# Filling TensorE's waits with unread products, and three changes of order, in a two-layer MoE network on one core

## The chip, the cores and the metric

The kernel runs on one core of a Trainium2 chip. The metric is device time of one execution in microseconds (us), lower is better. PE is TensorE (matrix products and transposes), DVE is VectorE, ACT is ScalarE, POOL is GpSimd, and SP is SyncE, which here only issues DMA transfers.

## The reference

Five hundred and twelve tokens of width 1024 pass through two layers and then two further blocks:

```python
for layer in range(DEPTH):                       # DEPTH = 2
    mix = gdn_mixer(h, ...) if layer == 0 else nsa_mixer(h, shared, ...)
    h = layer_norm(DEEPNORM_ALPHA * h + mix, ...)
    ffn = hier_moe(h, ...)                       # 16 experts, hidden 256, top 2
    h = layer_norm(DEEPNORM_ALPHA * h + ffn, ...)
x = second_block(h, ...)                         # twice: SGU, MLA, band attention, gated sum

def hier_moe(x, w_grp, b_grp, w_rt, b_rt, w_gate, w_up, w_down):
    grp_p = softmax(xt @ w_grp + b_grp)          # 4 groups: take the best
    e_logits = (xt @ w_rt + b_rt)[best group]    # 4 experts in it: take two
    gate = ...                                   # weights of the two, zeros elsewhere
    for wg, wu, wd, ge in experts:
        acc += ge[:, None] * ((silu(xt @ wg) * (xt @ wu)) @ wd)
```

## The kernel before

All weights are read from HBM in pieces of 512 KB (`chunk`, line 98), issued by SP into a ring of raw tiles; where a stage has spare tiles they are lent to the ring. Each piece is split into two reduced-precision parts: `hi` by an ACT cast (line 109) and `lo` by a DVE subtraction (line 110; in the experts POOL does it for the last of the four pieces of the first product, `c == 3`). Three matmuls (lines 114 to 116, or line 973 in the experts) then give the product of full precision. PE's stages follow one another without a choice: a tile scheduler keeps the written order of each engine except where priorities or `issue_after` move a row, and semaphores tie the engines together.

The start: SP loads the transposed input (`xT`, eight pieces, line 1761), a few constants, and the first mixer weights `g_w`. POOL builds a table of attention biases in `XT` with 32 small copies (line 1124), and SP writes it back to HBM as `n_fwd` (line 1126). PE first multiplies by the small weights `g_ab` (result in `br`), then by `g_w` (`mm<-xh,hi`).

Each layer's MoE: the logits of four token tiles (line 753, 128 x 20, eight of them a tile, each two PE instructions in the trace) go to DVE, where `dispatch` finds two experts per token (mask `M`, line 791), ranks, and the table `itok` of token numbers per expert. POOL gathers the rows of an expert by indirect DMA (`xr<-hd`, line 927), PE transposes them (line 189), and the branch of line 863 skips an overflow path. Every expert has a first product (`up`, four pieces), silu and product (lines 977 and 978, tile `sg`), a transpose of `sg`, and a second product (`down`, two pieces, results `yo`), which POOL adds to `acc` in HBM by an indirect DMA (`scatter`, line 932). PE runs `up(e)` before `down(e-1)`. Every scatter waits for the one before to land. The last two experts' results do not go by HBM: `combine` multiplies them by one-hot matrices (line 1054), adds `acc` (line 1057), and normalizes.

PSUM banks are shared by tag: four for `mm`, two each for `tp` and `br`.

Of the kernel before, what the change touches and what calls it, by code (L numbers as in the profile page):

```python
# [10 lines left out]
F32 = mybir.dt.float32  # L11
F32R = mybir.dt.float32r
BF = mybir.dt.bfloat16
I32 = mybir.dt.int32
U32 = mybir.dt.uint32
AF = mybir.ActivationFunctionType
OP = mybir.AluOpType
# [48 lines left out]
class Net:  # L66
    def __init__(self, ctx, tc, I, out, dbg):
# [12 lines left out]
        self.pows = self.cst.tile([128, 32], F32, name="pows")  # L80
        nc.vector.memset(self.pows, -0.5)
        self.flip = self.turn = self.turn2 = 0
        self.more, self.pairs = [], []
# [42 lines left out]
    def psum(self, tag="mm", shape=(128, 512), dtype=F32):  # L126
        return self.ps.tile(list(shape), dtype, name=tag, tag=tag, bufs=self.banks[tag])

    def copy(self, dst, src):
# [574 lines left out]
class Moe:  # L704


    def __init__(self, net, cx, l):
        self.net, self.l = net, l
        nc, tc = net.nc, net.tc
        self.mp = mp = cx.enter_context(tc.tile_pool(name="moe", bufs=1))  # L710
        self.wr = mp.tile([128, 160], F32, name="wr")
        nc.gpsimd.dma_start(self.wr, net.I[f"m_r{l}"])
        self.br = mp.tile([128, 20], F32, name="br")
# [8 lines left out]
        self.ws = mp.tile([128, 16], F32, name="ws")  # L722
        self.slots = net.psum("br")
        self.hT = []
# [25 lines left out]
    def logits(self, t):  # L750
        net = self.net
        for k in range(8):
            net.nc.tensor.matmul(self.slots[:, 64 + t * 20:84 + t * 20], lhsT=self.hT[t][:, k], rhs=self.wr[:, k * 20:k * 20 + 20],
                                 start=k == 0, stop=k == 7)

    def dispatch(self):
# [10 lines left out]
        def first_max(src, oh):  # L767
# [13 lines left out]
        x, e2, o1, o2 = (s(NT, 5, 4) for _ in range(4))  # L781
        V.tensor_tensor(x.rearrange("p t g e -> p t (g e)"), self.slots[:, 64:144].rearrange("p (t c) -> p t c", c=20),
                        self.br.unsqueeze(1).to_broadcast([128, NT, 20]), op=OP.add)
# [4 lines left out]
        for k, o in enumerate((o1, o2)):  # L788
            V.tensor_tensor(self.E2[:, k].rearrange("p t (g e) -> p t g e", e=4), o[:, :, 1:5],
                            og.unsqueeze(3).to_broadcast([128, NT, 4, 4]), op=OP.mult)  # L790
        V.tensor_tensor(self.M, self.E2[:, 0], self.E2[:, 1], op=OP.add)
        rk = net.psum("br", (128, NT, 128))
        for t in range(NT):
            for u in range(t + 1):
                PE.matmul(rk[:, t, :16], lhsT=net.ones_bf if u < t else net.tri_bf, rhs=self.M[:, u],
                          start=u == 0, stop=u == t)

        cv = self.cv
# [48 lines left out]
    def overflow(self):  # L847
# [5 lines left out]
        for u in range(NT):  # L853
            PE.matmul(cp[:, :16], lhsT=net.ones_bf, rhs=self.M[:, u], start=u == 0, stop=u == NT - 1)
        cm = mp.tile([128, 1], F32, name="cmx")
        V.tensor_reduce(cm, cp[:, :16], axis=AX.X, op=OP.max)
# [95 lines left out]
    def experts(self, aside=lambda: None):  # L952
        net, mp = self.net, self.mp
        nc = net.nc
        V, S, G, PE = nc.vector, nc.scalar, nc.gpsimd, nc.tensor
# [3 lines left out]
        def operand(k, tag, src, ps="tp"):  # L959
# [5 lines left out]
            return h, l, [lambda b=b: step(b) for b in range(0, k, 4)]  # L965

        def up(e, xh, xl, steps):

            pg = net.psum()
            for c in range(4):  # L970
                hi, lo = net.chunk(w[e, c], eng=G if c == 3 else None)
                for j, (a, b, k) in enumerate([(xh, hi, 0), (xl, hi, 0), (xh, hi, 1), (xl, hi, 1), (xh, lo, 0), (xh, lo, 1)]):
                    PE.matmul(pg, lhsT=a[:, c * 2 + k], rhs=b[:, k * 512:k * 512 + 512], start=c + j == 0, stop=c == 3 and j == 5)  # L973
                if steps:
                    steps.pop(0)()
            sg = mp.tile([128, 256], F32, name="sg", tag="sg", bufs=2)
            S.activation(sg, pg[:, :256], AF.Silu)
            V.tensor_tensor(sg, sg, pg[:, 256:512], op=OP.mult)
            return operand(2, "h", sg, "br")

        def down(e, hh, hl):
# [7 lines left out]
            for c in range(2):  # L989
                cs = slice(c * 512, c * 512 + 512)  # L990
                hi, lo = net.chunk(w[e, 4 + c])
                py = net.psum()
# [20 lines left out]

        self.ys, self.ots = [], []
        with net.longer(*self.places()):
            self.rows(XR - 1)
            x = [operand(8, "xe", self.xr[0])]
            for s in x[0][2]:
# [19 lines left out]
    def combine(self, done):  # L1038
# [9 lines left out]
        for t, r in enumerate(rt):  # L1048
            sm2, sm, ss, rs = small("sm2", 2), small("sm"), small("ss"), small("rs")
            ps = [net.psum() for _ in range(2)]  # L1050
            for j, (ot, y) in enumerate(zip(self.ots, self.ys)):
                for c in range(2):
                    for i in range(2):
                        PE.matmul(ps[c], lhsT=ot[:, t], rhs=y[i][:, c * 512:c * 512 + 512], start=j + i == 0, stop=j == DIRECT - 1 and i == 1)
            for c in range(2):
                cs = slice(c * 512, c * 512 + 512)
                V.scalar_tensor_tensor(r[:, cs], ps[c], 1.0, r[:, cs], op0=OP.mult, op1=OP.add, accum_out=sm2[:, c:c + 1])
# [681 lines left out]
def tile_network(ctx: ExitStack, tc: tile.TileContext, I, out, dbg=()):  # L1739
# [15 lines left out]
    xt = net.xt_pair()  # L1755
    net.phase(mm=4, tp=2, br=2)
    g_small = gdn_small(net)
    for j in range(4):
        xx = net.ring.tile([128, RING], F32, name="raw", tag="raw", bufs=RAW)
        for u in range(2):  # L1760
            nc.sync.dma_start(xx[:, u * T:u * T + T], I["xT"][2 * j + u])
        v = xx.rearrange("p (k t) -> p k t", k=2)
# [52 lines left out]
```

## Time and profile before

| | before |
|---|---|
| median of 3 runs | 2187.76 us (2184.25 to 2189.46) |
| profiled execution, time | 2186.32 us |
| profiled execution, span | 2184.6 us |
| mean granted TensorE clock | 0.974 |
| busy: PE, DVE, ACT, POOL | 2081.1, 1427.6, 1118.6, 367.6 us |
| span in which PE was not busy (2184.6 less 2081.1) | 103.5 us |

The page gives busy times over the span; the granted clock is the share of TensorE's full rate (1.00 is 2.4 GHz, 0.50 is 1.2 GHz). A timeline row reads: start, busy time, engine, line and operation, tile written from tiles read, count, and in brackets how long the engine had stood idle and what released it. Rows with SPq are DMA issues by SP.

### The profile page before, as it was taken

Reading aid. Unit: us, or ns where it says so; the run is one execution under the profiler, and the core shown is the slowest. Engines: PE = TensorE matmul, PEld = TensorE weight load, DVE = VectorE, ACT = ScalarE, POOL = GpSimd, SP = SyncE. Lnnn points to the kernel's source line nnn. Section 1 sums busy time; section 2 is a strip of 40 time slices with the busy share of each in tenths; the row PEclk is TensorE's granted clock in tenths of the full one; section 3 lists DMA queues with packets and bytes.
Section 4 is the critical chain, followed back from the end, with each engine's and each line's share of the span. In section 5 each row is a group of like instructions: output and inputs, shape, how many; then the busy total and the mean of one; then the engine's idle time right before and its main releaser. Section 6 shows DMA issues by size and latency. Waiting matters only on the chain.

```text
span 2184.6 us, 30258 instructions
## 1 busy us (share of the span) xinstructions
PE 2081.1 (95%) x10657; PEld 1662.7 (76%) x10657; DVE 1427.6 (65%) x2898; ACT 1118.6 (51%) x2234; POOL 367.6 (17%) x363
## 2 busy tenths in 40 slices
PE   8999988999999989799899999999999999999998
PEld 6777876887777657688678877777878887777786
DVE  6787667898548886699965555555456556455544
ACT  4545442997337874398643344454244324445432
POOL 4411023553200001365420010000011001000000
PEclk9998998999999999799999999999999999999999
DMA  6334437998441103799756454334435646433442
GB/s 208 100 131 124 148 101 259 351 326 281 173 134 60 49 20 127 264 345 328 261 166 197 155 174 149 116 106 150 146 109 171 202 135 186 128 119 111 150 151 74
DMA packets 134414, 365.09 MB, mean 167 GB/s; under 512 B 28608, under 2 KB 41328, under 8 KB 132464
## 3 DMA queue, kind: packets, MB, share of 16 engines
q1 hardware_dynamic: 81024, 271.65, 37.0%
q0 software_dynamic: 19776, 54.85, 8.0%
q10 hardware_dynamic: 33456, 36.59, 5.5%
q8 instruction: 86, 1.41, 0.3%
q14 instruction: 72, 0.59, 0.1%
HBM read 314.40 MB, written 64.61 MB: 173 GB/s over the span
## 4 chain that ended last, share of the span: by engine, by line
PE 45%; DMA 4%; DVE 4%; issue 3%; ACT 1%; POOL 1%; DVEq 0%; POOLq 0%; SPq 0%; ACTq 0%
PE mm L114 8%; PE mm L116 7%; PE mm L115 7%; PE br L114 5%; PE br L116 5%; PE br L115 5%; PE tp L189 2%; DMA raw<-in_m_w_dram 2%; PE mm L1619 2%; PE mm L973 2%; DMA xh<-in_m_w_dram 1%; DVE lo L110 1%; DMA xl<-in_m_w_dram 1%; ACT hi L109 1%; DMA qk<-qkd 1%
## 5 line engine op out<-in xcount | busy, mean ns | idle before, releaser
L110 DVE TENSOR_TENSOR lo<-raw,hi 128x1024 fp32r<-128x1024 f32 x266 | 338.5, 1276 | 297.3 <-ACT hi L109 294.6
L109 ACT CAST hi<-raw 128x1024 fp32r<-128x1024 f32 x276 | 288.5, 1047 | 418.3 <-PE mm L115 146.2
L114 PE MATMUL mm<-xh,hi 128*128 128x512 f32 x688 | 273.1, 397 | 2.1 <-DVE acc L323 2.1
L115 PE MATMUL mm<-xl,hi 128*128 128x512 f32 x688 | 271.2, 394 | 0.0
L116 PE MATMUL mm<-xh,lo 128*128 128x512 f32 x688 | 270.5, 394 | 0.4 <-DVE lo L110 0.3
L114 PE MATMUL mm<-hi,xh 128*128 128x512 f32 (+1 forms) x480 | 189.2, 394 | 4.9 <-ACT xh L109 4.2
L116 PE MATMUL mm<-hi,xl 128*128 128x512 f32 (+1 forms) x480 | 188.5, 393 | 1.6 <-DVE xl L110 1.5
L114 PE MATMUL br<-xh,hi 128*128 128x512 f32 x464 | 186.0, 401 | 2.2 <-DVE tm L1604 1.9
L115 PE MATMUL br<-xl,hi 128*128 128x512 f32 x464 | 187.8, 405 | 0.0
L115 PE MATMUL mm<-lo,xh 128*128 128x512 f32 (+1 forms) x480 | 187.8, 391 | 0.0
L116 PE MATMUL br<-xh,lo 128*128 128x512 f32 x464 | 184.4, 398 | 0.0
L1153 ACT ACTIVATE s<-s,mx 128x128 f32<-128x128 f32 (+3 forms) x256 | 143.5, 563 | 23.6 <-DVE mx L1151 22.9
L114 PEld LDWEIGHTS mm<-xh,hi 128*128 128x128 f32 x688 | 130.9, 190 | 29.6 <-issue 2.8
L116 PEld LDWEIGHTS mm<-xh,lo 128*128 128x128 f32 x688 | 130.4, 190 | 29.2 <-DVE lo L110 2.0
L115 PEld LDWEIGHTS mm<-xl,hi 128*128 128x128 f32 x688 | 130.6, 190 | 26.7
L1160 ACT COPY PT<-tp 128x128 f32<-128x128 f32 (+3 forms) x256 | 102.7, 423 | 24.1 <-PE tp L189 23.5
L973 PE MATMUL mm<-hi,xeh 128*128 128x512 f32 x256 | 110.2, 431 | 0.0
L114 PEld LDWEIGHTS mm<-hi,xh 128*128 128x128 f32 x480 | 91.3, 190 | 24.6 <-ACT xh L109 5.6
L189 PE MATMUL tp<-call,s 128*128 128x128 f32 x640 | 107.3, 277 | 2.0 <-ACT PT L1160 0.9
L116 PEld LDWEIGHTS mm<-hi,xl 128*128 128x128 f32 x480 | 91.3, 190 | 21.5 <-DVE xl L110 3.8
L115 PEld LDWEIGHTS mm<-lo,xh 128*128 128x128 f32 x480 | 91.3, 190 | 17.6 <-issue 0.2
L114 PEld LDWEIGHTS br<-xh,hi 128*128 128x128 f32 x464 | 87.8, 189 | 21.2 <-issue 3.2
(510 smaller groups left out, 4493.9 us busy)
## 6 DMA issues: line engine op xcount, KB each, us to landing
raw<-in_s_w_dram SPq DMA_DIRECT2D x128, 512.0 KB, 3.6
raw<-in_m_w_dram SPq DMA_DIRECT2D x48, 512.0 KB, 11.2
xh<-in_m_w_dram SPq DMA_DIRECT2D x44, 512.0 KB, 12.0
raw<-in_g_w_dram SPq DMA_DIRECT2D x40, 512.0 KB, 3.7
xl<-in_m_w_dram SPq DMA_DIRECT2D x40, 512.0 KB, 12.8
raw<-in_n_w_dram SPq DMA_DIRECT2D x32, 512.0 KB, 4.4
ho<-in_m_w_dram SPq DMA_DIRECT2D x24, 512.0 KB, 8.9
raw<-in_s_br_dram SPq DMA_DIRECT2D x24, 512.0 KB, 3.4
```

The costliest lines, as they stand in the source:

```text
L109: self.nc.scalar.copy(hi, src)
L110: (eng or self.nc.vector).tensor_tensor(lo, src, hi.bitcast(F32), op=OP.subtract)
L114: mm(ps, lhsT=ah, rhs=bh, start=start, stop=False)
L115: mm(ps, lhsT=ah, rhs=bl, start=False, stop=False)
L116: mm(ps, lhsT=al, rhs=bh, start=False, stop=stop)
L189: self.nc.tensor.transpose(tp[:, j], src(b + j), self.ident)
L973: PE.matmul(pg, lhsT=a[:, c * 2 + k], rhs=b[:, k * 512:k * 512 + 512], start=c + j == 0, stop=c == 3 and j == 5)
L1153: S.activation(p[:, :n], s[:, :n], AF.Exp, bias=mx, scale=-1.0, accum_out=sm)
L1160: S.copy(PT[:, t:4 * t + 1:3], tp)
L1619: PE.matmul(o[u_ * 64:u_ * 64 + 64, jt * 128:], lhsT=vt[:, jt, h * 64:h * 64 + 64], rhs=pt_rhs(PTs[u_], jt), start=jt == 0, stop=jt == NT - 1)
```

## The change

A helper `idle(n)` issues n matmuls of a bf16 tile of ones (128 columns of weights, 512 columns streamed) into a PSUM bank whose content nobody reads. They are called at the start (14), in each layer's dispatch (15 ahead of the mask's use, 5, 6) and before the first expert's transposes (8), and in the second layer's combine (16). The logits get a bank of their own and stream 128 columns, of which 20 are read; the weight tile is widened to 268 columns, and POOL clears the added 108. The casts of the pieces 1 to 3 of `up(e)` are issued after the silu and the product of `up(e-1)`, and so are those of the last `down`. Every second piece of the input is issued by ACT in place of SP.

```diff
+        self.one = self.cst.tile([128, 128], BF, name="one")
+        nc.vector.memset(self.one, 1.0)
...
+    def idle(self, n, tag="tp"):
+
+        ps = self.psum(tag, (128, 4, 128))
+        for _ in range(n):
+            self.tc.keep_in_program_order(self.nc.tensor.matmul(
+                ps, lhsT=self.one, rhs=self.one.unsqueeze(1).to_broadcast([128, 4, 128]), start=True, stop=True))
...
-        self.wr = mp.tile([128, 160], F32, name="wr")
-        nc.gpsimd.dma_start(self.wr, net.I[f"m_r{l}"])
+        self.wr = mp.tile([128, 268], F32, name="wr")
+        nc.gpsimd.memset(self.wr[:, 160:], 0.0)
+        nc.gpsimd.dma_start(self.wr[:, :160], net.I[f"m_r{l}"])
...
-            net.nc.tensor.matmul(self.slots[:, 64 + t * 20:84 + t * 20], lhsT=self.hT[t][:, k], rhs=self.wr[:, k * 20:k * 20 + 20],
+            net.nc.tensor.matmul(self.lg[:, t], lhsT=self.hT[t][:, k], rhs=self.wr[:, k * 20:k * 20 + 128],
...
+        net.idle(15)
+        V.tensor_tensor(x.rearrange("p t g e -> p t (g e)"), self.lg[:, :, :20],
...
+        net.idle(5)
 
         cv = self.cv
...
             PE.matmul(cp[:, :16], lhsT=net.ones_bf, rhs=self.M[:, u], start=u == 0, stop=u == NT - 1)
+        net.idle(6)
...
+        def behind(ins):
+
+            cx = ExitStack()
+            for i in ins:
+                cx.enter_context(tc.issue_after(i.ins))
+            return cx
...
-                hi, lo = net.chunk(w[e, c], eng=G if c == 3 else None)
+                with behind(self.gated if c else ()):
+                    hi, lo = net.chunk(w[e, c], eng=G if c == 3 else None)
...
-            S.activation(sg, pg[:, :256], AF.Silu)
-            V.tensor_tensor(sg, sg, pg[:, 256:512], op=OP.mult)
+            self.gated = (S.activation(sg, pg[:, :256], AF.Silu), V.tensor_tensor(sg, sg, pg[:, 256:512], op=OP.mult))
...
-                hi, lo = net.chunk(w[e, 4 + c])
+                with behind(self.gated if e == n - 1 else ()):
+                    hi, lo = net.chunk(w[e, 4 + c])
...
             self.rows(XR - 1)
+            net.idle(8)
...
+            if self.l and t == 1:
+                net.idle(16)
...
+    net.idle(14)
     g_small = gdn_small(net)
...
-            nc.sync.dma_start(xx[:, u * T:u * T + T], I["xT"][2 * j + u])
+            (nc.scalar if u else nc.sync).dma_start(xx[:, u * T:u * T + T], I["xT"][2 * j + u])
```

The order on SP at the start, of the kernel before (each row: line, operation, tile written from what is read, shape, count):

```order
L236 DMA raw<-in_g_ab_dram 128x128
L1761 DMA raw<-in_xT_dram 128x512 x8
L87 DMA call<-in_cst_dram 128x512
L254 DMA row<-in_g_row_dram 128x144
L256 DMA nw<-in_g_row_dram 128x1
L280 DMA cw<-in_g_cw_dram 128x96
L98 DMA raw<-in_g_w_dram 128x1024 x4
L1126 DMA n_fwd<-XT 16x1040
L1127 DMA s_fwd<-XT 16x640
```

And the same place of the changed kernel, whose lines stand 2 to 26 further down in the file:

```order
L245 DMA raw<-in_g_ab_dram 128x128
L1787 DMA raw<-in_xT_dram 128x512 x3
L89 DMA call<-in_cst_dram 128x512
L263 DMA row<-in_g_row_dram 128x144
L265 DMA nw<-in_g_row_dram 128x1
L1787 DMA raw<-in_xT_dram 128x512
L289 DMA cw<-in_g_cw_dram 128x96
L1151 DMA n_fwd<-XT 16x1040
L100 DMA raw<-in_g_w_dram 128x1024 x4
L1152 DMA s_fwd<-XT 16x640
```

Beside the four input pieces that left for ACT, the bias table `n_fwd`, which waits for POOL's copies, now stands ahead of the first four pieces of `g_w`.

On POOL, in the first experts of layer 0, the kernel before has the subtraction for expert e+2 ahead of the scatter of expert e:

```order
L110 TENSOR_TENSOR lo<-xl,hi 128x1024
L932 DMA acc_2941<-yo,itok 512x1024
L927 DMA xr_2942<-hd_2940,itok 128x1024
L110 TENSOR_TENSOR lo<-raw,hi 128x1024
L932 DMA acc_2941<-yo,itok 512x1024
L927 DMA xr_2943<-hd_2940,itok 128x1024
```

In the changed kernel, from the first scatter on:

```order
L946 DMA acc_2959<-yo,itok 512x1024
L112 TENSOR_TENSOR lo<-xl,hi 128x1024
L941 DMA xr_2960<-hd_2958,itok 128x1024
L946 DMA acc_2959<-yo,itok 512x1024
L112 TENSOR_TENSOR lo<-raw,hi 128x1024
L941 DMA xr_2961<-hd_2958,itok 128x1024
```

The scatter of expert e now stands ahead of the subtraction for expert e+2, here and through the stage.

On ACT, at the end of layer 0's experts, the kernel before has both casts of the last `down` (tile `ho`) ahead of the last silu (`sg`):

```order
L109 CAST hi<-raw 128x1024
L109 CAST hi<-ho 128x1024
L109 CAST hi_2948<-ho 128x1024
L977 ACTIVATE sg<-mm 128x256
L996 ACTIVATE xeh<-mm,ws 128x512
```

In the changed kernel:

```order
L999 ACTIVATE sg<-mm 128x256
L111 CAST hi<-ho 128x1024
L111 CAST hi_2966<-ho 128x1024
L1018 ACTIVATE xeh<-mm,ws 128x512 x2
L111 CAST hh<-br 128x256
```

The last silu now comes first and the casts of `ho` stand behind it.

## Rows read from the trace of the kernel before

**Rows 1.** The page's busy times: us, share of the span, instructions.

```profile
PE 2081.1 (95%) x10657; PEld 1662.7 (76%) x10657; DVE 1427.6 (65%) x2898; ACT 1118.6 (51%) x2234; POOL 367.6 (17%) x363
```

**Rows 2.** Timeline of the start, all engines.

```profile
8.21 4.72 SPq L98 DMA_DIRECT2D raw<-in_g_w_dram  x4
9.68 6.46 POOL L1124 COPY XT<-XT 16x1 f32<-16x1 f32 x32 [2.54 <-DMA XT<-in_n_rel_dram]
...
12.64 1.05 ACT L109 CAST hi<-raw 128x1024 fp32r<-128x1024 f32 x1 [1.21 <-DMA raw<-in_g_w_dram]
...
15.27 0.39 PE L115 MATMUL br<-xl,pg 128*16 128x512 f32 x1
...
15.50 0.40 PE L116 MATMUL br<-xh,pg 128*16 128x512 f32 x1
...
16.16 0.34 SPq L1126 DMA_DIRECT2D n_fwd<-XT  x1
...
17.01 0.50 PE L114 MATMUL mm<-xh,hi 128*128 128x512 f32 x1
```

**Rows 3.** The page's DMA issues: KB each, median us to landing.

```profile
raw<-in_g_w_dram SPq DMA_DIRECT2D x40, 512.0 KB, 3.7
```

**Rows 4.** Windows, layer 0's dispatch: PE busy, granted clock, DMA share, GB/s.

```profile
362.00:364.00 2.00, 2.00 (x12) 0.50 1.04 422
...
382.00:384.00 2.00, 2.00 (x12) 0.98 0.92 350
```

**Rows 5.** Timeline of layer 0's dispatch, PE.

```profile
357.83 3.17 PE L753 MATMUL br<-wr,hT 128*128 128x20 f32 x27
...
362.50 3.54 PE L753 MATMUL br<-wr,hT 128*128 128x20 f32 x16
...
369.92 0.42 PE L795 MATMUL br<-M,cb 128*128 128x16 bf16 x10 [3.88 <-DVE M L791]
...
378.06 0.66 PE L189 MATMUL tp<-call,xr 128*128 128x128 f32 x2 [4.36 <-DVEq L863]
```

**Rows 6.** Timeline of layer 1's dispatch, PE.

```profile
889.84 5.68 PE L753 MATMUL br<-wr,hT 128*128 128x20 f32 x30
...
895.35 1.95 PE L189 MATMUL tp<-call,r 128*128 128x128 f32 x8
...
897.30 3.60 PE L753 MATMUL br<-wr,hT 128*128 128x20 f32 x16
...
913.34 0.66 PE L189 MATMUL tp<-call,xr 128*128 128x128 f32 x2 [4.79 <-DMA xr<-hd,itok]
```

**Rows 7.** Window of layer 1's first expert, columns as above.

```profile
920.00:922.00 2.00, 2.00 (x8) 0.66 1.00 387
```

**Rows 8.** PE's timeline in layer 0's experts, first and ninth.

```profile
399.37 0.38 PE L189 MATMUL br<-call,sg 128*128 128x128 f32 x2
...
475.32 0.38 PE L189 MATMUL br<-call,sg 128*128 128x128 f32 x2
```

**Rows 9.** POOL's timeline in layer 0's experts, first and last scatter.

```profile
398.52 2.41 POOL L110 TENSOR_TENSOR lo<-xl,hi 128x1024 fp32r<-128x1024 f32 x1 [3.33 <-ACT hi L109]
401.08 2.44 POOL L932 DMA_INDIRECT acc<-yo,itok  x1 [0.16 <-issue]
...
532.12 1.60 POOL L932 DMA_INDIRECT acc<-yo,itok  x1 [3.52 <-DMA acc<-yo,itok]
```

**Rows 10.** Timeline of the end of layer 0's experts.

```profile
532.92 0.38 ACT L977 ACTIVATE sg<-mm 128x256 f32<-128x256 f32 x1
...
534.66 0.44 PE L189 MATMUL br<-call,sg 128*128 128x128 f32 x2 [2.01 <-DVE sg L978]
...
536.36 0.80 PE L114 MATMUL mm<-hi,hh 128*128 128x512 f32 x1 [1.26 <-ACT hh L109]
```

**Rows 11.** Window of that end, columns as above.

```profile
538.00:540.00 2.00, 2.00 (x7) 0.50 0.03 6
```

**Rows 12.** Timeline of layer 1's combine, PE.

```profile
1088.33 1.73 PE L189 MATMUL tp<-call,xn 128*128 128x128 f32 x8 [5.02 <-DVE rs L1061]
```

More of the change, by code (lines that the diff above doesn't have):

```diff
@@ L722, in __init__ @@
         self.ws = mp.tile([128, 16], F32, name="ws")
-        self.slots = net.psum("br")
+        self.lg = net.psum("br", (128, NT, 128))
         self.hT = []
@@ L781, in dispatch @@
         x, e2, o1, o2 = (s(NT, 5, 4) for _ in range(4))
-        V.tensor_tensor(x.rearrange("p t g e -> p t (g e)"), self.slots[:, 64:144].rearrange("p (t c) -> p t c", c=20),
+        net.idle(15)
+        V.tensor_tensor(x.rearrange("p t g e -> p t (g e)"), self.lg[:, :, :20],
                         self.br.unsqueeze(1).to_broadcast([128, NT, 20]), op=OP.add)
@@ L791, in dispatch @@
         V.tensor_tensor(self.M, self.E2[:, 0], self.E2[:, 1], op=OP.add)
+        self.slots = net.psum("br")
         rk = net.psum("br", (128, NT, 128))
@@ L953, in experts @@
         net, mp = self.net, self.mp
-        nc = net.nc
+        nc, tc = net.nc, net.tc
         V, S, G, PE = nc.vector, nc.scalar, nc.gpsimd, nc.tensor
@@ L1012, in place @@
             self.ots.append(ot)
-        self.ys, self.ots = [], []
+        self.ys, self.ots, self.gated = [], [], ()
         with net.longer(*self.places()):
             self.rows(XR - 1)
+            net.idle(8)
             x = [operand(8, "xe", self.xr[0])]
```

## The prediction

> **What bounds it.** I read the busy times first: PE works 95% of the span [rows 1], so what can be won lies in 103.5 us of gaps and in the stretches in which its work runs at the lower clock. Second, the clock by windows of 2 us: in layer 0's dispatch it stands at 0.50 in 362 to 364 although PE is busy all the time, and only in 382 to 384 is it back at 0.98 [rows 4]; in layer 1 it is still recovering in 920 to 922 [rows 7], and at the end of layer 0's experts it is 0.50 again [rows 11]. Third, the timelines at these places and at the start, for what PE waits for there. The reader is to see in them that most gaps are short and end by another engine's chain: a filled gap brings nothing by itself, only by the clock of the work behind it. Fourth, POOL's timeline in the experts, because the diff's `behind` turns its order round.
>
> **Price of an unread product.** Two matmuls of 512 columns start 0.23 us apart at full clock (15.27 and 15.50) [rows 2]. At the low clock I take the ratio of the logits: 16 in 3.54 us are 0.221 each, 27 in 3.17 are 0.117 [rows 5], a factor 1.88, so 0.43. The wider logits I take as free: at the low clock eight 128-column transposes took 1.95 us, 0.244 each, and sixteen 20-column logits 3.60, 0.225 each [rows 6]; from both sides 0 to 0.02 x 64, 1.3 us a layer. The memsets of `one` and of the weight tile lie on DVE and POOL long before their readers: nothing.
>
> **The start.** Before, the first `g_w` piece was in by 12.64, and PE started on it at 17.01 because the 24 products by `g_ab` ran until then [rows 2]. The 14 idles are meant for those, but SP's order decides. `n_fwd` waits for POOL's copies, which end at 9.68 + 6.46 = 16.14, and was issued at 16.16 [rows 2]. It now stands ahead of all `g_w` pieces, so the first of them is issued at 16.16 + 0.34 = 16.5, lands 3.7 later [rows 3], is cast in 1.05 [rows 2], and PE starts at 21.3: 4.3 us late. Queued behind this wait on SP are four weight pieces; PE, ACT and DVE wait for them. The landing is at least 512 KB at 422 GB/s [rows 4], 1.2 us, and at most what the piece issued at 8.21 needed until 12.64, 4.4 [rows 2]: +1.8 to +5.0. I stay with the median, since by then the inputs are in. PE then stands some 5 us between the two products, and its clock can fall: work worth up to 3 us extra, as layer 1's dispatch shows below. I take 0.7 of that: **+5.0**. Two queues for the input save SP four issues and nothing else; it waits for POOL anyway. The Trainium skill ("DMA: Bandwidth & Descriptors", "Issuing engines are not separate DMA queues") says that spreading transfers over engines saves only the issuer's time, not bandwidth; no row here shows two queues for one load. By it the sum would be the same, by a gain in bandwidth it would be too, because the weights come last.
>
> **Layer 0's dispatch.** If the clock holds, the last 16 logits take 16 x 0.117 = 1.9 in place of 3.54: -1.7. The transposes ahead of them (eight, at the low clock 1.95 [rows 6], half at full) give -0.8 of what ran slowly. Idle(15) is 15 x 0.23 = 3.45 in a wait of 3.88 [rows 5]: covered; without that cover, at 0.43, it is 6.45 and costs 2.6. Behind it DVE's chain stays as it is. The six ahead of the branch (1.4) and the eight between branch and transposes (1.84) stand in and behind a wait of 4.36 that the branch ends, not PE [rows 5]: the eight are paid in full, the six I take at 1.0. From 378.06 to 382 the work ran slowly: 3.9 us to 2.0, -1.9. Sum -1.7 - 0.8 - 1.9 + 1.84 + 1.0 = **-1.5**; if the clock is low, 2.6 + 2 x 1.84 less nothing, so up to +6.
>
> **Layer 1's dispatch.** The low stretch starts earlier, so more work lies in it: 30 logits in 5.68 become 3.5 (-2.2, of which the rows to be transposed allow 2.0), eight transposes 1.95 become 1.0, sixteen logits 3.60 become 1.9 [rows 6]: -4.7 for DVE's start. The transposes of the first expert waited 4.79 for the gather [rows 6], which hides nearly all idles there: +0.6. Its slow work from 913.34 until about 921 [rows 6, 7], 7.7 us with some 6 busy: -2.9. The gather now runs while the stage's loads still fill the DMA engines (share 1.04 in layer 0 at that point [rows 4]): +0.5. Sum **-6.5**, and +1 if the clock stays low.
>
> **Experts.** PE needs (475.32 - 399.37) / 8 = 9.49 us an expert [rows 8]; the scatters start (532.12 - 401.08) / 13 = 10.08 apart, because each waits for the last to land [rows 9]. Before, this chain trailed behind PE and stopped nothing, since the subtraction for e+2 stood ahead of it. Now that subtraction stands behind the scatter, so PE's `up` comes to wait for the chain: 0.59 an expert once its slack is used up, which I estimate to take half of the 14: 4.5 us. In exchange the first scatter no longer stands behind 2.41 us of `lo` [rows 9], and since the chain's end sets when `combine` can read `acc`, layer 0's end comes 2.4 earlier. PE's own end is earlier too: the last silu, at 532.92, had stood behind a cast that waited for its weights; PE waited 2.01 and 1.26 [rows 10] and then ran at 0.50 [rows 11] for about 6 us, 3 too many. That is 6.3 won against 4.5 lost, -1.8. The chain's -2.4 and PE's -1.8 are near enough; I take **-2.4**. Layer 1 had no such wait at its end, so the 4.5 is paid less what the chain's earlier start gives: **+1.5**, bounds -1 and +4.5.
>
> **Layer 1's combine.** 16 x 0.23 = 3.7 us go into a wait of 5.02 [rows 12]. The transposes behind it took 1.73 for eight and would take 1.0, and the products after them ran slowly for a time. The order moves eleven matmuls (2.5 us) behind the last transposes, which gives most of it back: **-1.0**, bounds -3 and +2.
>
> **Sum.** +5.0 - 1.5 - 6.5 - 2.4 + 1.5 - 1.0 = -4.9, made against the profiled execution: 2186.32 - 4.9 = 2181.4. The median of the runs is 1.44 higher, which makes 2182.9; I say 2182.
>
> **Rivals.**
> *The clock does not hold.* The clock fell at 362 under work without a gap [rows 4], so filled time alone is not proof. Then idle(15) costs 2.6 and the eight 3.4 per layer where nothing hides them: layer 0 +6, layer 1 +1, start +6, the ends -0.9, combine +1: +13 at worst, +6 if it fails in one layer. The point from which it decides: a granted clock at 0.50 when the logits end. The transposes speak for it: the stretch that fell consists of them and logits. The Trainium skill ("TensorE: Matmul & The Clock Gate", "Part 4: PE-mode transpose") says that transposes don't count as busy in the way products do. The trace agrees as far as its fall at 362 goes. Time: 2192. 0.18.
> *POOL's chain sets PE's pace and gives nothing back* (the other side): if the first scatter starts no earlier, because `yo` is late too, each layer's stage is 4.5 longer and layer 0's end wins only 1.8: +5.0 - 1.5 - 6.5 + 2.7 + 4.5 - 1.0 = +3.2, 2189.5. It decides when the scatters' spacing stays at 10 and PE waits for `lo` of POOL in most experts. For it: 10.08 against 9.49. Against it: POOL's row at 401.08 followed its subtraction by 0.16 us [rows 9], so that was what held it. 0.17.
> *The gains come and the losses don't.* POOL's copies end sooner, or the start's clock holds (+2), the experts keep PE's pace (layer 0's end -6.3 as far as the chain lets it, -4; layer 1 0), combine -2: +2 - 1.5 - 6.5 - 4 + 0 - 2 = -12, 2174. 0.22.
> *It does nothing*: the fills hold the clock but every place then waits for DVE, POOL or DMA until the old time, and the start costs what the dispatches give: 2186. 0.08.
>
> **Chances.** The sum as worked out has 0.35, with -9 to 0 as its own range. A measurement of this kernel can tell about 0.2%, 4.4 us, from no change. The sum lies just beyond: of its 0.35, 0.21 is faster and 0.14 same. With 0.22 of the third rival and 0.04 of the others' luckier ends, faster has 0.47. Same: 0.14, the last rival's 0.07, 0.06 of the others: 0.27. Slower 0.26, from the first two. The range goes from the third rival's end, 2170, to the first one's single failure with the second's, 2194.
>
> **What would show it.** Start: `n_fwd` issued near 16, the first product by `g_w` near 21; at 14 the step is wrong. Dispatch: a clock of 1.00 through both, DVE's first row of layer 1 4 to 5 us nearer to the last `r`. Experts: the scatters' spacing, PE's waits for POOL's `lo`, and no wait of PE at `sg` and `hh` at layer 0's end. Combine: a clock of 1.00 after the gap. The forecast falls most easily by the start's size and by what POOL's new order does to PE's pace.

## The result and the profile after

The changed kernel took 2206.48 us (median of 6 runs, 2203.53 to 2215.17) against 2184.24 of the kernel before (6 runs, the first three of which are those shown ahead): a ratio of 1.0104, 95% interval 1.0081 to 1.0127. It is slower by 1%, outside the predicted range and on the other side of it. The profiled execution took 2203.53 us with a span of 2201.8, 17.2 us above the span of before; the comparisons below go by spans and rows of one profiled execution each, the verdicts by medians.

The page's busy times:

```profile
PE 2101.6 (95%) x10755; PEld 1649.9 (75%) x10755; DVE 1458.6 (66%) x2899; ACT 1118.3 (51%) x2234; POOL 372.1 (17%) x365
```

PE is still busy 95% of the span [rows 1], with 98 matmuls more, whose results nobody reads. Its busy time rose by 20.5 us, so the page alone would say that nothing waits more than before. The mean granted clock rose from 0.974 to 0.987. A better clock and a worse time: the loss has to be searched by stages.

The start, from the timeline of all engines:

```profile
14.47 0.39 PE L118 MATMUL br<-xh,pg 128*16 128x512 f32 x1
15.27 0.34 SPq L1151 DMA_DIRECT2D n_fwd<-XT  x1
15.72 2.02 SPq L100 DMA_DIRECT2D raw<-in_g_w_dram  x4
...
20.89 0.80 PE L116 MATMUL mm<-xh,hi 128*128 128x512 f32 x1 [6.03 <-ACT hi L111]
...
25.29 0.63 PE L117 MATMUL mm<-xl,hi 128*128 128x512 f32 x1
25.71 0.45 PE L118 MATMUL mm<-xh,lo 128*128 128x512 f32 x1
26.00 0.40 PE L116 MATMUL mm<-xh,hi 128*128 128x512 f32 x1
```

The idles did their part: the products by `g_ab` ended 1 us sooner than in [rows 2]. But `n_fwd` waited for POOL until 15.27, four weight pieces stood behind it on SP, and PE waited 6.03 us and started 3.9 us late (20.89 against 17.01), at the low clock: matmuls of 0.63 until 25.7, then of 0.40.

The windows of layer 0's dispatch, columns as in [rows 4]:

```profile
368.00:370.00 2.00, 2.00 (x18) 1.00 1.06 383
370.00:372.00 2.00, 2.00 (x11) 1.00 0.98 311
...
376.00:378.00 2.00, 1.07 (x10) 0.85 1.03 420
378.00:380.00 2.00, 1.99 (x5) 0.50 1.01 416
...
386.00:388.00 2.00, 1.95 (x9) 0.59 0.81 215
```

and PE's rows there:

```profile
377.31 2.67 PE L135 MATMUL tp<-one 128*128 128x512 bf16 x6
381.78 1.04 PE L135 MATMUL tp<-one 128*128 128x512 bf16 x2 [1.80 <-DVEq L877]
382.61 0.53 PE L856 MATMUL br<-q,sl 128*128 128x48 bf16 x8
382.96 2.73 PE L135 MATMUL tp<-one 128*128 128x512 bf16 x6
385.49 1.92 PE L198 MATMUL tp<-call,xr 128*128 128x128 f32 x8
```

The clock held through the logits and the long DVE chain, where it stood at 0.50 before, and fell at the short matmuls in front of the branch. So the eight idles that stand behind it ran at the low clock: they are the rows of 2 and of 6, and the transposes started 3.7 us after the first of them (381.78 to 385.49) instead of 1.84. The gather came later too. It was issued at 377.70 and landed 6.1 us later, at 383.8; before, it was issued at 373.93 and took 3.3. So the first expert's transposes came 7.4 us later than in [rows 5]: 3.7 of that were there at the branch (381.78 against 378.06), and of the other 3.7 at most 1.7 (383.8 to 385.49) is owed to the idles alone. In layer 1 the clock held until 920, the first transposes still waited for the gather, which was issued at 916.21:

```profile
920.22 2.73 PE L135 MATMUL tp<-one 128*128 128x512 bf16 x6
923.75 1.09 PE L198 MATMUL tp<-call,xr 128*128 128x128 f32 x8 [0.80 <-DMA xr<-hd,itok]
```

They started 7.5 us after the gather's issue; in the kernel before it was 4.6 (issued at 908.71, started at 913.34 [rows 6]). The DMA engines were full there: share 1.03 and 1.03 in 916 to 920, where the kernel before had 0.28 in 908 to 912. SP now has two more pieces of weights ahead of the branch.

The experts, from POOL's timeline:

```profile
407.71 1.64 POOL L946 DMA_INDIRECT acc<-yo,itok  x1 [4.99 <-ACT yo L1018]
...
458.37 2.22 POOL L946 DMA_INDIRECT acc<-yo,itok  x1 [3.60 <-DMA xl<-in_m_w_dram]
460.05 2.96 POOL L112 TENSOR_TENSOR lo<-pg,hi 128x1024 fp32r<-128x1024 f32 x1
...
468.65 2.19 POOL L946 DMA_INDIRECT acc<-yo,itok  x1 [3.63 <-DMA acc<-yo,itok]
```

and what PE, ACT and PE again do with it, in the timeline of all engines:

```profile
463.09 0.70 PE L995 MATMUL mm<-lo,xeh 128*128 128x512 f32 x2
...
463.63 0.39 PE L116 MATMUL mm<-hi,hh 128*128 128x512 f32 x1
...
467.12 0.69 ACT L1018 ACTIVATE yo<-mm,ws 128x512 f32<-128x512 f32 x1 [0.43 <-PE mm L118]
```

This can be read off row by row: a scatter is issued (458.37), the subtraction behind it starts 1.7 us later and takes 2.96, so it is done at 463.01; PE's last two products of the expert, which read it, start at 463.09; the second product of the expert before starts at 463.63, its result `yo` is written by 467.81, and the next scatter goes at 468.65. From scatter to scatter these are 10.3 us, and PE's own work for an expert is 9.49 [rows 8]. In the kernel before the subtraction was ahead of the scatter [rows 9], so PE did not wait for a scatter.

A scatter waits for two things, its `yo` and the landing of the scatter before, and the bracket names only one. Which of the two came last can be read from the distances. In the kernel before `yo` was written long ahead, and the scatter started 0.8 us behind the landing: the one of 452.11 took 9.3 us to land, at 461.4, the next one started at 462.20, and its `yo` was written by 455.93.

```profile
452.11 1.60 POOL L932 DMA_INDIRECT acc<-yo,itok  x1 [3.72 <-ACT xeh L109]
...
462.20 2.57 POOL L932 DMA_INDIRECT acc<-yo,itok  x1 [4.32 <-DMA acc<-yo,itok]
```

Where `yo` alone was missing, as for the first scatter of the changed kernel (407.71, `yo` written by 407.43), it started 0.3 us behind `yo`. In the middle of the changed kernel's stage the distances are those of a landing, each time:

| scatter starts | the one before landed (its start + its time to landing) | `yo` written by |
|---|---|---|
| 438.46 | 427.90 + 9.8 = 437.7 | 436.90 |
| 448.61 | 438.46 + 9.4 = 447.9 | 447.30 |
| 458.37 | 448.61 + 9.0 = 457.6 | 457.56 |
| 468.65 | 458.37 + 9.5 = 467.9 | 467.81 |
| 479.43 | 468.65 + 10.0 = 478.7 | 478.08 |
| 489.37 | 479.43 + 9.2 = 488.6 | 488.34 |
| 499.62 | 489.37 + 9.5 = 498.9 | 498.60 |

So the chain of scatters sets the pace, 10.25 us a scatter from 427.90 to 499.62, and hands it to PE through the subtraction behind it. The way round through PE and ACT is closed as well, but shorter: `yo` at 467.81 and 0.3 behind it would have let the scatter go 9.7 us after the one before.

PE's waits for POOL's `lo` in this whole stage sum to only 2.2 us in three places; the rest hides in matmuls that start 0.33 to 0.54 us apart instead of 0.23 (457.37 and 457.70; 463.63, 464.16 and 464.50).

Two more losses stand beside the pace. From the transpose of the first `sg` to that of the second it takes 11.33 us (396.60 to 407.93) where it was 7.94, because the second expert's casts now wait for the first silu:

```profile
398.87 0.50 PE L995 MATMUL mm<-hi,xeh 128*128 128x512 f32 x1 [0.48 <-ACT hi L111]
...
402.77 0.73 PE L995 MATMUL mm<-lo,xeh 128*128 128x512 f32 x2 [0.88 <-POOL lo L112]
...
505.16 0.73 PE L995 MATMUL mm<-lo,xeh 128*128 128x512 f32 x2 [2.71 <-DVE lo L112]
```

The last of these rows is PE's longest wait of the stage, ahead of the twelfth `sg`: DVE's two subtractions in front of it (from 500.67) took 5.57 us, while POOL did its own from 501.08 to 504.02.

The combine of layer 1:

```profile
1108.24 1.97 PE L198 MATMUL tp<-call,xn 128*128 128x128 f32 x8 [5.02 <-DVE rs L1086]
...
1111.82 5.00 PE L135 MATMUL tp<-one 128*128 128x512 bf16 x16 [0.62 <-DVE xl L112]
```

The sixteen idles did not go into the wait of 5.02 us [rows 12]. The wait is there as before, and the idles ran behind it and behind the first transposes, partly at the low clock, for 5.00 us. The granted clock was 0.50 in 1108 to 1112.

### The profile page after: what moved, and what is told of

Read it like the earlier page. It is cut to its first block, busy times and chain, and to the rows that moved or that the text cites. A ratio compares the mean times of both kernels' runs of the same rounds, so it can differ in the third digit from the quotient of the medians.

```text
span 2201.8 us, 30378 instructions
## 1 busy us (share of the span) xinstructions
PE 2101.6 (95%) x10755; PEld 1649.9 (75%) x10755; DVE 1458.6 (66%) x2899; ACT 1118.3 (51%) x2234; POOL 372.1 (17%) x365
## 4 chain that ended last, share of the span: by engine, by line
PE 59%; DVE 10%; DMA 5%; ACT 4%; issue 3%; POOL 1%; DVEq 0%; POOLq 0%; ACTq 0%; SPq 0%
PE mm L117 10%; PE mm L116 10%; PE mm L118 10%; PE br L116 6%; PE br L118 6%; PE br L117 6%; DVE lo L112 5%; PE tp L198 4%; ACT hi L111 2%; PE mm L1644 2%; PE mm L1364 1%; PE mm L995 1%; DMA hT<-in_m_w_dram 1%; DMA xh<-in_m_w_dram 1%; PE mm L1358 1%
## 5 line engine op out<-in xcount | busy, mean ns | idle before, releaser
L112 DVE TENSOR_TENSOR lo<-raw,hi 128x1024 fp32r<-128x1024 f32 x266 | 346.2, 1307 | 304.3 <-ACT hi L111 302.4
L1178 ACT ACTIVATE s<-s,mx 128x128 f32<-128x128 f32 (+3 forms) x256 | 143.4, 562 | 22.1 <-DVE mx L1176 21.4
L117 PEld LDWEIGHTS mm<-lo,xh 128*128 128x128 f32 x480 | 91.0, 190 | 17.6 <-issue 0.2
```

The source lines that it names most:

```text
L112: (eng or self.nc.vector).tensor_tensor(lo, src, hi.bitcast(F32), op=OP.subtract)
L117: mm(ps, lhsT=ah, rhs=bl, start=False, stop=False)
L1178: S.activation(p[:, :n], s[:, :n], AF.Exp, bias=mx, scale=-1.0, accum_out=sm)
```

## The experiments

Twelve kernels were run, in three batches. Each batch has its own runs of the kernel before (medians 2184.34, 2185.77 and 2184.61 us), to which the ratios belong. The first four take the change's casts apart: all of it but the casts, the casts alone, the casts with POOL's old order, and POOL's new order without the casts.

**Without the casts behind the silu.**

```diff
-            self.gated = (S.activation(sg, pg[:, :256], AF.Silu), V.tensor_tensor(sg, sg, pg[:, 256:512], op=OP.mult))
+            S.activation(sg, pg[:, :256], AF.Silu)
+            V.tensor_tensor(sg, sg, pg[:, 256:512], op=OP.mult)
```

> The changed kernel without the casts put behind the silu; all else as changed. Theory A (the casts behind the silu slow the experts, from 5.2 us late at the first transpose of sg to 13.0 at the first row of layer 0's combine, and from 5.5 to 19.8 in layer 1): without them layer 0's combine starts 5 us later than in the kernel before, layer 1's experts 3 us earlier, and the whole ends 3 to 6 us below the kernel before, some 22 us below the changed one. Rival B (the experts are slow because the earlier loads or the idles upset the transfers): it stays within 5 us of the changed kernel, with 10.2 us an expert.

Measured: 2186.02 us, ratio 1.0009 (0.9994 to 1.0023), span 2181.4. Theory A holds in the main: 20.5 us of the loss are the casts' part, and the rest of the change cannot be told from nothing. The 3 to 6 us below the kernel before that it also forecast are not there.

**The casts behind the silu alone.** The kernel before with `behind`, `gated` and the two `with` lines of the change's diff.

> The kernel before with nothing but the casts put behind the silu. Theory A: 8 us lost in layer 0's experts and 14 in layer 1's, so 18 to 24 us slower than before, with 10.2 us an expert. Rival B: within 4 us of before, 9.5 us an expert.

Measured: 2208.67 us, ratio 1.0117 (1.0094 to 1.0141), 24.3 us above the kernel before. Theory A again, from the other side.

**The casts behind the silu, POOL's order as before.** The scatter of an expert is recorded after the first product of the expert two later, and behind its subtraction (the lines that keep the subtraction as `lo4` are left out):

```diff
-                self.scatter(yo, self.itok[:, e:e + 1])
+                self.late.append((yo, self.itok[:, e:e + 1]))
...
                 hs.append(up(e, *x[e][:2], steps))
+                for late in self.late:
+                    with tc.issue_after(self.lo4.ins):
+                        self.scatter(*late)
+                self.late = []
```

> The changed kernel with the casts behind the silu kept, but each scatter on POOL put back behind the subtraction for the expert two later, as in the kernel before. Theory A1 (it is POOL's order, the subtraction behind a scatter that waits for the last to land): 9.5 us an expert and some 20 us below the changed kernel. Theory A2 (it is ACT and DVE, which get the casts later than PE can use them): 10.2 us an expert and within 5 us of the changed kernel.

Measured: 2192.18 us, ratio 1.0029 (1.0014 to 1.0044). It falls between the two: 14.3 us below the changed kernel, but 6.2 above the run without the casts' part. A1 has the larger share and A2 the smaller. In POOL's timeline of this run the subtraction is ahead of the scatter again, and the scatter waits for nothing but the landing:

```profile
456.24 2.56 POOL L112 TENSOR_TENSOR lo<-pg,hi 128x1024 fp32r<-128x1024 f32 x1 [3.28 <-ACT hi L111]
459.52 1.83 POOL L946 DMA_INDIRECT acc<-yo,itok  x1 [0.72 <-DMA acc<-yo,itok]
...
465.72 2.82 POOL L112 TENSOR_TENSOR lo<-xl,hi 128x1024 fp32r<-128x1024 f32 x1 [3.03 <-ACT hi L111]
469.01 2.08 POOL L946 DMA_INDIRECT acc<-yo,itok  x1 [0.47 <-DMA acc<-yo,itok]
```

**POOL's new order alone.** The kernel before, with the subtraction behind the scatter and ACT as it was (the lines that keep the scatters in `sc` are left out):

```diff
-                hi, lo = net.chunk(w[e, c], eng=G if c == 3 else None)
+                with net.tc.issue_after(self.sc[-1].ins) if c == 3 and self.sc else ExitStack():
+                    hi, lo = net.chunk(w[e, c], eng=G if c == 3 else None)
```

> The kernel before with only POOL's order changed: each subtraction for the expert two later stands behind the scatter; the casts on ACT are not held back. Theory A1: 10 us an expert and 10 to 20 us slower than before. Theory A2: within 4 us of before.

Measured: 2208.96 us, ratio 1.0117 (1.0089 to 1.0144), 24.6 us above the kernel before, more than the 10 to 20 of Theory A1. One edge on an engine that is busy 17% of the span costs as much as the whole change. Its POOL rows have the order of the changed kernel:

```profile
463.47 1.86 POOL L932 DMA_INDIRECT acc<-yo,itok  x1 [3.62 <-ACT hi L109]
464.81 2.97 POOL L110 TENSOR_TENSOR lo<-xl,hi 128x1024 fp32r<-128x1024 f32 x1
```

Here twelve of the two layers' 28 scatters start 0.28 us behind their `yo`, so these waited for PE's result and not for the chain; in the changed kernel there are seven. That the order alone costs 24.6 and only 14.3 of the changed kernel's 20.5 says that the two parts don't add; why is not shown.

What the profiles of these runs say of layer 0's experts, in us; the third and fourth columns are starts of rows of PE as in [rows 8], the last is the first row of DVE in the combine:

| kernel | first product by the mixer weights | second `sg` transpose | tenth | an expert, difference over 8 | first row of the combine |
|---|---|---|---|---|---|
| before | 17.01 | 399.37 | 475.32 | 9.49 | 544.92 |
| changed | 20.89 | 407.93 | 489.04 | 10.14 | 557.90 |
| without the casts' part | 20.96 | 404.13 | 480.79 | 9.58 | 548.77 |
| casts' part alone | 16.18 | 400.46 | 480.81 | 10.04 | 550.62 |
| casts' part, POOL's old order | 20.92 | 407.05 | 484.11 | 9.63 | 551.86 |
| POOL's new order alone | 16.14 | 400.48 | 483.76 | 10.41 | 552.02 |

(The two rows of [rows 8] are the second and the tenth of their stage.) The pace follows POOL's order and not the casts on ACT. What stays with POOL's old order is paid ahead of it. From the first transpose of `sg` to the second it is 11.3 to 11.4 us in both layers of all three kernels that hold the casts back, and 7.9 in the three that don't. Some of that is won before: from the first expert's first product to the second transpose of `sg` it is 20.7 us with the casts held back (386.37 to 407.05) and 18.9 without (385.24 to 404.13), and in layer 1 22.1 (922.61 to 944.71) against 18.6 (915.04 to 933.63), though the clock differs there too.

**The bias tables written by POOL.** From here on all kernels are built on the first run, without the casts' part.

```diff
-    nc.sync.dma_start(net.n_fwd, fwd)
-    nc.sync.dma_start(net.s_fwd, sf)
+    G.dma_start(net.n_fwd, fwd)
+    G.dma_start(net.s_fwd, sf)
```

> As the run without the casts behind the silu, and the two bias tables are written back by POOL, which makes them, in place of SP, so that no weight stands behind them. Theory A (the wait on SP in front of the weights is all that the start costs): the first product by the mixer weights moves from 20.9 to 14 or 15, and the time falls by 5 to 7 us against that run. Rival B (the weights would be late anyway, by the transfers at the start): it moves by less than 2 and the time by less than 2.

Measured: 2178.86 us, ratio 0.9971 (0.9958 to 0.9984), 7.2 us below the run without it (8.3 by the ratios, as the batches differ). The start in its timeline:

```profile
7.40 10.80 SPq L100 DMA_DIRECT2D raw<-in_g_w_dram  x6
...
15.01 0.78 PE L116 MATMUL mm<-xh,hi 128*128 128x512 f32 x1 [0.54 <-ACT hi L111]
```

The weights are issued at 7.40 and PE starts on them at 15.01. Theory A. This is the best kernel of the study, 0.3% faster than the kernel before.

**Logits of 20 columns.**

```diff
-            net.nc.tensor.matmul(self.lg[:, t], lhsT=self.hT[t][:, k], rhs=self.wr[:, k * 20:k * 20 + 128],
+            net.nc.tensor.matmul(self.lg[:, t, :20], lhsT=self.hT[t][:, k], rhs=self.wr[:, k * 20:k * 20 + 20],
```

> As the run without the casts behind the silu, but the logits stream 20 columns as in the kernel before; the idles stay. Theory A (the wide logits are what keeps the clock up while they run): the granted clock falls to 0.50 before the idles, in layer 1 for the 30 logits too, and DVE's first row after them comes 2 us later in layer 0 and 4 to 5 in layer 1. Rival B (idles elsewhere hold the clock, the width is without effect): both come as early, and the time is the same within 2 us.

Measured: 2189.61 us, ratio 1.0017 (1.0001 to 1.0033), 3.6 above the run with wide logits; by the ratios it is 1.7, not clear of noise. The windows of layer 1's logits:

```profile
896.00:900.00 4.00, 4.00 (x23) 0.54 1.03 420
900.00:904.00 4.00, 4.00 (x19) 0.50 0.97 336
904.00:908.00 4.00, 4.00 (x12) 0.50 1.03 415
908.00:912.00 4.00, 4.00 (x23) 0.76 0.64 262
```

PE is busy without a gap and the clock falls all the same, as in the kernel before [rows 4]; with 128 columns it stood at 1.00 here. DVE's first row after the logits comes 1.6 us later in layer 0 and 6.5 in layer 1, of which 3.3 were there before layer 1. Theory A, by the rows and the clock.

**No idles in the dispatch** (15, 5, 6 and 8 deleted, the wide logits kept).

```diff
-        net.idle(15)
...
-        net.idle(5)
...
-        net.idle(6)
...
-            net.idle(8)
```

> As the run without the casts behind the silu, with the wide logits, but without the idles of the dispatch and before the first expert (15, 5, 6 and 8). Theory A (they cost as much as they give, because they stand between the branch and the first transposes): first transposes of layer 0 2 to 4 us earlier, the first expert's matmuls 2 slower, the time within 2 us. Rival B (they are worth their price): 3 us or more slower.

Measured: 2188.37 us, ratio 1.0009 (0.9998 to 1.0021), 2.4 above the run with them, within the spread of both; the ratios are equal. The clock fell, as it should without them (windows of layer 1):

```profile
896.00:900.00 4.00, 2.58 (x20) 1.00 1.03 352
900.00:904.00 4.00, 0.41 (x10) 0.60 1.00 394
...
916.00:920.00 4.00, 4.00 (x21) 0.50 0.44 151
```

but the first transposes were no earlier where the prediction has the idles in their way:

```profile
383.34 0.66 PE L198 MATMUL tp<-call,xr 128*128 128x128 f32 x2 [7.60 <-DMA ho<-in_m_w_dram]
```

PE waited 7.60 us instead of running idles, and started 0.6 us earlier than with them. What ended the wait was the gather: it was issued at 375.96 and landed 7.2 us later, at 383.2. So in layer 0 the idles cost 0.6 here and not the 2.8 of the prediction, because they stand in front of a landing, and the first transpose of `sg` comes 1.1 later without them; in layer 1 it comes 4.0 later. The times decide for neither theory.

**The last down's casts alone behind the last silu, and the tables by POOL.**

```diff
-                with behind(self.gated if c else ()):
-                    hi, lo = net.chunk(w[e, c], eng=G if c == 3 else None)
+                hi, lo = net.chunk(w[e, c], eng=G if c == 3 else None)
```

> The tables written by POOL, and of the casts only those of the last down behind the last silu; the other casts and POOL's order as before; all else as changed. Theory A: the start's 6 us and some 3 at the end of layer 0's experts come on top of the run without the casts: 2176 to 2179, which is 0.25 to 0.5% below the kernel before. Rival B (the end of the stage hangs on the chain of scatters, whatever ACT does first): no more than the start's gain, 2180.

Measured: 2182.46 us, ratio 0.9983 (0.9970 to 0.9996), not below the run with the tables alone, 2178.86. In layer 0 it gains: from the transpose of the first `sg` (392.22) to the first row of the combine (543.37) it is 151.15, against 152.65 with the tables alone (389.07 to 541.72). That is 1.5 us and not 3 (the eight kernels that have this stage without the silu's new place, the one with the tables among them, lie between 152.0 and 152.9), and it is lost among the runs. Rival B is nearer, and a row says why: the combine now waits for `acc`, which is read back behind the last scatter.

```profile
543.37 0.69 DVE L1081 SCALAR_TENSOR_TENSOR r<-mm,r 128x512 f32<-128x512 f32 x1 [1.84 <-DMA r<-acc]
```

**Three parts taken from the run with the tables by POOL**, and the eight idles before the first expert:

```diff
-            if self.l and t == 1:
-                net.idle(16)
...
-    net.idle(14)
...
-            (nc.scalar if u else nc.sync).dma_start(xx[:, u * T:u * T + T], I["xT"][2 * j + u])
+            nc.sync.dma_start(xx[:, u * T:u * T + T], I["xT"][2 * j + u])
...
-            net.idle(8)
```

(one kernel each)

> As the run with the tables written by POOL, without the 16 idles of layer 1's combine. Theory A (they hold the clock there and give 1 to 3 us, less what the eleven matmuls moved behind the last transposes cost): 0 to 2 us slower, with a granted clock of 0.50 after the gap of 5 us. Rival B (they give nothing because DVE's chain sets the pace of the combine): the same within 1 us.

> As the run with the tables written by POOL, without the 14 idles at the start. Theory A (with the weights early, the 24 products by g_ab at the low clock set the start again): the first product by the mixer weights near 17.0 in place of 15.0, 1 to 3 us slower. Rival B (the input's landing sets it): at 15.0, the same.

> As the run with the tables written by POOL, but all eight input pieces issued by SP as before. Theory A (the second queue saves issue time alone, and the last piece's issue on ACT comes late): the first product by the mixer weights within 1 us of 15.0, the time within 2 us. Rival B (two queues bring the input sooner): 2 us or more later.

> As the run with the tables written by POOL, without the 8 idles ahead of the first expert's transposes. Theory A (in layer 0 they stand in PE's way behind the branch, 1.9 us; in layer 1 the gather lands after them): layer 0's first transposes 1 to 2 us earlier, layer 1's as early, the work behind them at the low clock for 2 us or more: within 2 us. Rival B (they are what holds the clock for the first expert): 3 us or more slower.

Measured, in this order: 2182.77 (0.9991, 0.9980 to 1.0002), 2180.97 (0.9984, 0.9973 to 0.9995), 2179.15 (0.9973, 0.9962 to 0.9984) and 2182.84 us (0.9990, 0.9978 to 1.0002). The second queue is worth nothing. The 14 idles bring PE's first product by the mixer weights from 16.50 to 15.01, and 2.1 us of the median, within the spread. The 16 and the 8 each give some 4 us by the medians, more than Theory A allowed for either. The profiles don't settle where: that of the kernel without the 16 is already 5.5 us late at the last product that the combine reads, ahead of the place where they were taken out, and that of the kernel without the 8 has layer 0's first transposes 3.7 us later (380.64 against 376.93) and not earlier. Without the 16 the clock falls in the gap:

```profile
1084.00:1088.00 4.00, 0.00 (x0) 0.62 0.62 251
1088.00:1092.00 4.00, 2.96 (x10) 0.50 0.00 0
```

but it does so with them too (0.50 in 1080 to 1088 of the run with the tables by POOL), as they stand behind the gap there as well. From DVE's row of `r` just ahead of the gap to the first of `low` behind the stage it is 37.5 us with them (1076.30 to 1113.81) and 38.4 without (1082.07 to 1120.48), so 0.9 of the 4 us belong to this stage.

## Why the prediction was wrong

In this section a row is late by its start in the changed kernel less its start in the kernel before.

The step that failed is **Experts**. From the transpose of the first `sg` to the combine, layer 0 lost 7.8 (from 5.2 late to 13.0) where -2.4 stood, and layer 1 lost 14.3 (5.5 to 19.8) where +1.5 stood. The two together are 23 us of error, and the sum missed by 22.1 (17.2 of span against -4.9). The chain of scatters was there, and it came to set PE's pace, as the step had it. What failed is what was set against it, and what was put at nothing:

- **The chain's price** was somewhat small. "I estimate to take half of the 14: 4.5 us" (half of 14 times 0.59 is 4.1) became 5.5 in layer 0, from the fourth `sg` to the eleventh (8.6 late to 14.1), and 5.8 in layer 1, from the third to the eleventh (8.9 to 14.7). The slack was used up after three or four experts, and the scatters came 10.25 apart and not 10.08.
- **Holding back the casts** was put at nothing. From the first `sg` to the second it cost 3.4 us in each layer, in every kernel that does it; 6.2 us of the whole, by the run with POOL's order put back.
- **DVE's subtractions beside POOL's** were put at nothing. With PE's wait of 2.71 at 505.16, the twelfth `sg` came another 2.9 late in layer 0, and 2.4 in layer 1.
- **"In exchange the first scatter no longer stands behind 2.41 us"**: where the order alone was changed, the first scatter came 0.7 us earlier (400.37 against 401.08), in the changed kernel 6.6 later (407.71), as it waits for `yo` and not for POOL.
- **The gain at layer 0's end** came, and not by the order that was to bring it. PE's waits of 2.01 and 1.26 [rows 10] became one of 0.82, the clock stood at 1.00 in 540 to 556, and 3.5 us were recovered between the last `sg` (16.5 late) and the combine (13.0 late). But the kernel with POOL's order alone, whose last silu stands where it stood before, is as quick there (545.69 to 552.02, 6.3 us, against 6.8 changed and 10.3 before). The silu's new place by itself gave 1.5.

The rest, step by step:
- **The start** was right. Predicted 21.3 for the first product, measured 20.89; predicted a low clock behind the wait, seen until 25.7. The run with the tables by POOL gave back 7.2 us: about the step's +5.0, and some 2 more because PE then starts at 15.01, ahead of the 17.01 of before.
- **Layer 0's dispatch** was right in that the clock holds through the logits and the mask's wait, and wrong at its end: it fell ahead of the branch, so the eight idles took 3.7 and not 1.84. From the transposes ahead of the logits (5.3 late, 353.92 and 359.25) to DVE's first row behind them (3.8 late, 366.08 and 369.90) 1.5 were won where the step had 2.5. Then the gather and the idles lost 3.6 (7.4 late at the first transposes), and the first expert's better clock gave 2.3. Of the -1.5 only 0.2 is left (5.2 late at the first `sg`).
- **Layer 1's dispatch**, -6.5, came near: the lateness fell from 11.7 at the transposes ahead of the logits (886.18 and 897.83) to 5.5 at the first `sg`, 6.2 us. Of it 4.1 were there at DVE's first row (908.48, 7.5 late), where the step had 4.7. The gather then lost 2.9 again (10.4 late at the first transposes), where the sum had 0.5 for the full DMA engines, and from there to the first `sg` the clock gave 4.9, more than the 2.9 of the step. So the step's sum came out by two errors that offset each other, which was luck.
- **The combine**, -1.0: 19.9 late at its last product, 17.6 behind the stage (DVE's row of `low`, 1120.96 and 1138.52), so -2.3. The reason given was wrong: the idles were not in the wait of 5.02, and its sign, a clock of 1.00 after the gap, was not seen.
- The rule of the Trainium skill on TensorE's clock ("TensorE: Matmul & The Clock Gate", "Part 4: PE-mode transpose"), on which the first rival leaned, is that transposes don't count as busy in the way products do. What transposes alone do to the clock no run here shows. The rival's fall at the logits did not come: the same transposes stand between the wide logits, and the clock held at 1.00; it fell when the logits alone were made narrow again.
- The rule of the Trainium skill on queues ("DMA: Bandwidth & Descriptors", "Issuing engines are not separate DMA queues") is that spreading transfers saves issue time and no bandwidth. The run with one input queue agrees: 0.3 us of difference.

The second rival, "POOL's chain sets PE's pace and gives nothing back", was the one that came, with 0.17 of the chance. Its signs, scatters that stay 10 us apart and a PE that waits for POOL's `lo`, are what the rows show. Its price for the pace, 4.5 a layer, was near the 5.5 and 5.8; it had the casts and DVE at nothing too, so its 2189.5 fell short as well.

## What to carry to other kernels

When an edit turns round two instructions on an engine that is mostly idle, follow both ends of each: if one belongs to a slow chain and the busiest engine needs the other, the chain's spacing becomes the pace, whatever the busy shares say. Price it by the longer of two ways, the chain's own spacing (here 10.25 us) and the way round through the other engines (here 9.7), and price apart what the edit holds back (here 3.4 us a layer). Then look where the scheduler put a filler: sixteen of them stood behind the gap that they were written for. And a transfer that waits for another engine belongs on the queue of that engine, where nothing urgent stands behind it: here that gave 7.2 us.

## What the runs showed of the hardware

- The granted clock fell with PE busy in every window of layer 1's logits at 20 columns (0.54, 0.50, 0.50 in 896 to 908) and stood at 1.00 with 128; the wide logits took 1.95 us for sixteen at full clock (360.13, line 763), 0.122 each, where 20-column ones took 0.117 [rows 5]. The columns nobody reads are nearly free.
- DVE's subtraction of a 128 x 1024 tile takes 1.2 us alone (1.23 at 20.87), and 3.94 with POOL's beside it. POOL's ran on for 2.84 us, and 2.84 + 1.2 is near 3.94, as if DVE had stood still meanwhile (an estimate from these rows):

```profile
460.05 2.96 POOL L112 TENSOR_TENSOR lo<-pg,hi 128x1024 fp32r<-128x1024 f32 x1
460.17 3.94 DVE L112 TENSOR_TENSOR lo<-xh,hi 128x1024 fp32r<-128x1024 f32 x1
```

- The time from a gather's issue to the transposes that read it went from 4.6 to 7.5 us when the DMA engines were at a share of 1.03 and not 0.28 (layer 1); the landing of layer 0's first gather went from 3.3 to 6.1.
- A scatter of 128 rows took 9.0 to 10.0 us from its issue to its landing in the rows of the table above. The next one started 0.7 to 0.8 us behind the landing, or 0.3 behind `yo` where that came last.
- What stays open: where the some 4 us of the 16 and of the 8 idles are won, and why POOL's order costs more alone than together with the casts.
